# Output projection in seven parts: spilled lo parts by other tiles and another queue, the last part on other banks, norm gains into pages of their own, and a set issue order

## The chip, the cores and the metric

The kernel runs on one core of a Trainium2 chip. TensorE multiplies matrices, VectorE, ScalarE and GpSimd do elementwise work, SyncE (SP) issues most of the DMAs between SBUF, the core's memory, and HBM. The metric is the time of one execution on the device in microseconds (us). The profile comes from one execution that a hardware profiler recorded.

## The reference

One layer of a decoder: three token mixers beside each other, merged by gates, and a gated MLP behind them. D_MODEL and SEQ are 1024, D_FF is 2816, all in fp32. Cut to the stretch that matters here:

```python
y_sb, y_ml, y_xa = ...             # three branches, each 1024 x 512
gates = jax.nn.sigmoid(gate_pre).reshape(bsz, seq, N_BRANCH, D_MODEL)
merged = (gates[:, :, 0] * (y_sb @ w_sb_out[l])
          + gates[:, :, 1] * (y_ml @ w_ml_out[l])
          + gates[:, :, 2] * (y_xa @ w_xa_out[l]))
x = x + merged @ w_o[l]
h = _rmsnorm(x, g_ffn[l])
u = _causal_dwconv(h @ w_up[l], ff_conv_w[l], ff_conv_b[l])
u_val, u_gate = jnp.split(u, 2, axis=-1)
x = x + (jax.nn.silu(u_gate) * u_val) @ w_down[l]
```

## The kernel before

Everything is kept transposed: channels on the 128 partitions, sequence along the free axis, in tiles of 128x1024 (or 128x512 halves). An fp32 product is made of three fp32r matmuls (`mm3`, L141 to L144: hi by hi, hi by lo, lo by hi), so each operand is split into hi and lo: `split` (L128 to L130) copies hi on ScalarE and subtracts lo on VectorE, or on an engine that is given. The larger products run in Strassen's manner, seven part products in place of eight, over sums and differences of quarters of the operands.

Tiles come from pools of rotating buffers by tag: `T(shape, "px")` waits until an earlier user of a px buffer is done. Tags that play a part here: raw, whi and wlo (a weight and its hi and lo), px, y, pg, h and U (general pages), `half()` (small tiles, hf in the profile). A scheduler orders the instructions of each engine by priority and by the data they need; each engine then runs its list in that order. `tc.high_priority` moves instructions ahead, `tc.issue_after` holds them behind a given one. PSUM has four tags of two banks each: pj and tr (LONG), pv and z (SHORT).

**The branches (L1115 to L1151).** 24 units i, eight for each of the three branches; b = i // 8. A unit has two halves of 12 matmuls each, accumulated in a bank pj. The weights `w_br` are loaded and split for two units together. VectorE evacuates each half: for branches 1 and 2, L1138 multiplies the bank by the gate, and L1139 adds the result to `merged`. The branch's four input tiles are loaded from y_d into px by SP (L1065) and split into h at the branch's first unit.

**The W_o sums (L1081 to L1099)** run beside branches 1 and 2, one step after each unit from unit 8 on. GpSimd makes the sums and differences of W_o's quarters, in pg (L1084, L1089, L1094, L1097), four for each of two column halves. `spill` (L1076 to L1079) then forms the sum's hi in a px tile on ScalarE, its lo in another px tile on GpSimd (L130), and SP stores the lo in HBM (slo_d, L1079). There are eight spills. Later `sum_w` (L1169 to L1173) makes hi anew on ScalarE and fetches lo from slo_d by a DMA on GpSimd's queue (L1172).

**The seven parts (L1226 to L1311).** `part_product` (L1157) yields after each of its four d; a d is 12 matmuls into one bank, a part 48. L is a quartet of banks on LONG's tags, R one on SHORT's. `grow` (L1186) adds a bank to an output tile (o1u, o2l, o2u, o1l). `squares` (L1195 to L1202) squares an output on ScalarE and adds it up on VectorE; `rstd` (L153 to L159, matmul L158) and `spread` (L161 to L169, matmul L168) turn the sums into a row of factors on all partitions. `gain` (L1208 to L1210) multiplies an output by g_ffn on ScalarE, in place. `keep` (L1188 to L1190) stores an output in x1_d (the profile calls it x_d). Part 6 accumulates on the chain's banks L; part 7 starts a fresh quartet R, so that o1l is grown from both L and R.

**The start of the FFN (L1335 to L1385)** multiplies the differences of the outputs by the second row of factors (L1206), forms operands t2, t3, t1, bl and t4 (L1354, L1363, L1369 and the splits), and runs the first units' parts in turn as operands come ready.

## Time and profile before

| | |
|---|---|
| runs | 1669.21, 1665.27, 1671.01 us; median 1669.21 |
| profiled execution | 1668.87 us, its span 1667.2 us |
| busy share of the span | TensorE 98%, weight loads 80%, VectorE 74%, ScalarE 50%, GpSimd 8% |
| HBM traffic | 159.86 MB read, 58.80 MB written |
| part products L1 to L7 | 939 to 1021 us in the span |

In rows of the profile, L is the line in the kernel before, PE is TensorE, PEld its weight loads, DVE VectorE, ACT ScalarE, POOL GpSimd. `out<-in` names tiles by their tags, with buffer numbers left out. In a timeline's row a bracket holds the idle time just before the instruction and what ended it. The matmuls overlap, so that a row's duration is longer than the step from start to start.

### The profile page before, as it was taken

Reading aid. Unit: us, or ns where it says so; the run is one execution under the profiler, and the core shown is the slowest. Engines: PE = TensorE matmul, PEld = TensorE weight load, DVE = VectorE, ACT = ScalarE, POOL = GpSimd, SP = SyncE. Lnnn points to the kernel's source line nnn. Section 1 sums busy time; section 2 is a strip of 40 time slices with the busy share of each in tenths; the row PEclk is TensorE's granted clock in tenths of the full one; section 3 lists DMA queues with packets and bytes.
Section 4 is the critical chain, followed back from the end, with each engine's and each line's share of the span. In section 5 each row is a group of like instructions: output and inputs, shape, how many; then the busy total and the mean of one; then the engine's idle time right before and its main releaser. Section 6 shows DMA issues by size and latency. Waiting matters only on the chain.

```text
span 1667.2 us, 21227 instructions
## 1 busy us (share of the span) xinstructions
PE 1627.1 (98%) x7959; PEld 1326.9 (80%) x7959; DVE 1234.3 (74%) x1673; ACT 838.5 (50%) x1278; POOL 140.7 (8%) x188
## 2 busy tenths in 40 slices
PE   8999999999999999999978999999999999999999
PEld 4878888888788888888856876788888888888887
DVE  5558888859665666676566868997778877789864
ACT  4557777546554455566222345564455554543431
POOL 1022222020000001000081000000000000000000
PEclk9999999999999999999988999999999999999999
DMA  8421011424325665336866444223222221486131
GB/s 297 149 65 33 26 39 64 174 79 152 116 101 171 190 184 161 118 123 227 269 212 217 124 136 133 83 101 101 77 76 76 85 95 61 161 319 240 41 136 70
DMA packets 102515, 220.05 MB, mean 132 GB/s; under 512 B 13384, under 2 KB 37256, under 8 KB 102412
## 3 DMA queue, kind: packets, MB, share of 16 engines
q1 hardware_dynamic: 101260, 214.50, 38.0%
q0 software_dynamic: 1152, 4.19, 1.0%
q8 instruction: 63, 1.03, 0.3%
q14 instruction: 40, 0.33, 0.1%
HBM read 159.86 MB, written 58.80 MB: 131 GB/s over the span
## 4 chain that ended last, share of the span: by engine, by line
PE 89%; DMA 4%; DVE 3%; ACT 2%; POOL 1%; issue 1%; SPq 0%; ACTq 0%; POOLq 0%; DVEq 0%
PE ps_pj L142 13%; PE ps_pj L143 12%; PE ps_pj L144 12%; PE ps_pv L144 5%; PE ps_pv L143 5%; PE ps_pv L142 5%; PE ps_tr L144 4%; PE ps_tr L142 4%; PE ps_tr L143 4%; PE ps_z L142 4%; PE ps_z L144 4%; PE ps_z L143 4%; PE ps_pv L440 2%; PE ps_tr L420 2%; PE ps_z L395 1%; PE ps_z L394 1%
## 5 line engine op out<-in xcount | busy, mean ns | idle before, releaser
L143 PE MATMUL ps_pj<-h,whi 128*128 128x512 f32 x520 | 206.1, 396 | 2.2 <-DVE h L130 2.0
L142 PE MATMUL ps_pj<-h,whi 128*128 128x512 f32 x440 | 179.0, 408 | 19.2 <-DVE U L1138 11.7
L129 ACT ACTIVATE whi<-raw 128x512 fp32r<-128x512 f32 (+1 forms) x101 | 82.5, 817 | 154.7 <-PE ps_pj L143 55.1
L144 PE MATMUL ps_pj<-h,wlo 128*128 128x512 f32 x352 | 139.1, 396 | 0.1
L143 PEld LDWEIGHTS ps_pj<-h,whi 128*128 128x128 f32 x520 | 99.0, 190 | 25.1 <-DVE h L130 5.9
L831 DVE SCALAR_TENSOR_TENSOR y<-U,vec,y 128x1023 f32<-128x1023 f32 x88 | 112.5, 1279 | 7.8 <-ACT y L829 7.8
L142 PEld LDWEIGHTS ps_pj<-h,whi 128*128 128x128 f32 x440 | 83.9, 191 | 40.1 <-DVE U L1138 13.3
L408 DVE TENSOR_TENSOR_SCAN U<-U 128x512 f32<-128x512 f32 (+3 forms) x96 | 92.9, 1009 | 22.1 <-POOL U L403 20.5
L142 PE MATMUL ps_pj<-pg,whi 128*128 128x512 f32 x268 | 104.5, 390 | 0.0
L144 PE MATMUL ps_pj<-pg,wlo 128*128 128x512 f32 x248 | 96.7, 390 | 0.0
L144 PEld LDWEIGHTS ps_pj<-h,wlo 128*128 128x128 f32 x352 | 67.2, 191 | 15.0 <-DVE wlo L130 0.6
L130 DVE TENSOR_TENSOR wlo<-raw,whi 128x1024 fp32r<-128x1024 f32 x44 | 54.4, 1235 | 29.4 <-ACT whi L129 29.3
L143 PE MATMUL ps_pv<-h,whi 128*128 128x512 f32 x190 | 73.9, 389 | 0.0
L143 PE MATMUL ps_pj<-pg,whi 128*128 128x512 f32 x188 | 73.4, 390 | 0.0
L129 ACT ACTIVATE whi<-pg 128x512 fp32r<-128x512 f32 (+1 forms) x46 | 35.3, 769 | 62.4 <-PE ps_z L143 18.2
L829 ACT ACTIVATE y<-U,vec 128x1024 f32<-128x1024 f32 x44 | 54.6, 1241 | 17.4 <-DVE U L722 16.9
L144 PE MATMUL ps_pj<-h,whi 128*128 128x512 f32 x160 | 62.6, 391 | 0.0
L144 PE MATMUL ps_pv<-h,wlo 128*128 128x512 f32 x152 | 59.5, 392 | 0.0
L142 PE MATMUL ps_pv<-h,whi 128*128 128x512 f32 x150 | 58.5, 390 | 0.4 <-DVE U L722 0.4
L142 PEld LDWEIGHTS ps_pj<-pg,whi 128*128 128x128 f32 x268 | 50.3, 188 | 10.2
L130 DVE TENSOR_TENSOR wlo<-raw,wlo 128x512 fp32r<-128x512 f32 x55 | 37.8, 687 | 26.6 <-ACT wlo L129 26.2
L397 ACT ACTIVATE U<-ps_z 128x1024 f32<-128x1024 f32 (+3 forms) x48 | 39.1, 814 | 32.0 <-PE ps_z L395 24.1
(492 smaller groups left out, 4550.1 us busy)
## 6 DMA issues: line engine op xcount, KB each, us to landing
raw<-in_w_t_dram SPq DMA_DIRECT2D x29, 512.0 KB
gate_d<-U SPq DMA_DIRECT2D x24, 512.0 KB
U<-gate_d SPq DMA_DIRECT2D x22, 512.0 KB
act_d<-y SPq DMA_DIRECT2D x22, 512.0 KB
pg<-in_w_t_dram SPq DMA_DIRECT2D x21, 512.0 KB
raw<-in_w_dn_dram SPq DMA_DIRECT2D x18, 512.0 KB
h<-act_d SPq DMA_DIRECT2D x14, 512.0 KB
raw<-in_w_br_dram SPq DMA_DIRECT2D x12, 512.0 KB
```

Source lines behind the costliest of these rows:

```text
L129: nc.scalar.activation(hi, src, AF.Copy)
L130: (eng or nc.vector).tensor_sub(lo, src, hi.bitcast(F32))
L142: nc.tensor.matmul(out, lh, rh, start=start, stop=False, skip_group_check=more)
L143: nc.tensor.matmul(out, lh, rl, start=False, stop=False, skip_group_check=more)
L144: nc.tensor.matmul(out, ll, rh, start=False, stop=stop, skip_group_check=more)
L394: nc.tensor.matmul(z[:, a, :w], qs[a][:, ts(rb)], ks[a][:, c], start=True, stop=False)
L397: nc.scalar.activation(f[:, :, 1:w + 1], z[:, :, :w], AF.Sigmoid, scale=-0.125)
L408: nc.vector.tensor_tensor_scan(f[:, a, 1:w + 1], f[:, a, 1:w + 1], f[:, a, 1:w + 1], 1.0 if o == 0 else f[:, a, 0:1], op0=ALU.mult, op1=AL ...
L420: nc.tensor.transpose(pt[:, a, ts(j)], g[:, a, ts(j)], ident)
L440: nc.tensor.matmul(pv[64 * a:64 * a + 64, ts(rb % 4)], sbv[s // 2][:, s % 2, (2 * p + a) * 64:(2 * p + a + 1) * 64], wt[a][:, ts(j)], star ...
L829: nc.scalar.activation(out, u, AF.Identity, bias=bias, scale=taps[0])
L831: nc.vector.scalar_tensor_tensor(out[:, :S - s], u[:, s:], taps[s], out[:, :S - s], op0=ALU.mult, op1=ALU.add)
```

## The change

Six edits, in the stretch from the W_o sums to the FFN's start:

1. `spill` takes its two tiles from tag y in place of px, and GpSimd's queue stores lo in place of SP's.
2. L and R change their banks (L on SHORT, R on LONG), and part 7 goes on accumulating on L in place of a fresh R. o1l is grown from part 7 alone, which holds both.
3. `gain` writes into pages of its own: `full` for the upper outputs, `blg` for o2l. The tile that is stored stays as it is.
4. The rstd matmuls of the upper half come after part 6's d = 1 (before: d = 0) and the spread after d = 3 (before: d = 1); the products with the rows and their splits go from part 6's and part 7's steps into part 7's alone.
5. The first FFN weights are loaded, summed and split ahead of part 6 (before: within part 7).
6. Grows and squares of parts 5 and 7 get priority; the parts' loops are written as `stage` and `ready`, which fetch the next part's weights after d = 1 and after the part (before: at d = 0 and d = 2).

The core of the diff:

```diff
@@ -1074,9 +1074,10 @@
     ws = [[None, None] for _ in range(4)]
 
     def spill(i, j):
-        hi, lo = T([P, S], "px", F32R), T([P, S], "px", F32R)
-        split(ws[i][j], hi, lo, nc.gpsimd)
-        nc.sync.dma_start(slo_d[i, j], lo.bitcast(F32))
+        hi, lo = T([P, S], "y", F32R), T([P, S], "y")
+        nc.scalar.activation(hi, ws[i][j], AF.Copy)
+        nc.gpsimd.tensor_sub(lo, ws[i][j], hi.bitcast(F32))
+        nc.gpsimd.dma_start(slo_d[i, j], lo)
 
     def wo_sums(j):
         a1, a2 = wo_load(0, 0, j, "pg"), wo_load(0, 1, j, "pg")
@@ -1205,68 +1209,77 @@
         v = t.rearrange("p (k r) -> p k r", k=2)
         op(v, v, rows.unsqueeze(1).to_broadcast([P, 2, HALF]))
 
-    def gain(o, i):
+    def gain(dst, o, i):
         for d in range(4):
-            nc.scalar.activation(part(o, d), part(o, d), AF.Copy, scale=col(C_GFFN + 4 * i + d))
-
-
-    L, R = four(LONG[::-1]), four(SHORT)
-    w2, w3, w4, w5, w6, w7 = ([None, None] for _ in range(6))
+            nc.scalar.activation(part(dst, d), part(o, d), AF.Copy, scale=col(C_GFFN + 4 * i + d))
 
     def operand(n, src):
         for j in range(2):
             m[n][j] = fine(src[j], "h")
 
+    L, R = four(SHORT), four(LONG)
+    weights = {1: w1}
+
+    def ready(n, j):
+        if n in (2, 5):
+            t = raw_w(1, n // 5, j)
+        else:
+            t = sum_w({3: 2, 4: 1, 6: 0, 7: 3}[n], j)
+        weights.setdefault(n, []).append(t)
+
+    def stage(n, banks, operand, start, after):
+        for d in part_product(banks, weights[n], operand, start):
+            if n < 7 and d == 1:
+                ready(n + 1, 0)
+            after(d)
+        if n < 7:
+            ready(n + 1, 1)
+
     o1u = out_tiles(0, 1, "U")
     operand("bu", bu)
     operand("t3", al)
-    for d in part_product(L, w1, "au", True):
-        if d % 2 == 0:
-            w2[d // 2] = raw_w(1, 0, d // 2)
-        grow(o1u, L, d)
+    stage(1, L, "au", True, lambda d: grow(o1u, L, d))
     operand("t2", au)
 
     o2l = out_tiles(1, 0, "px")
-    for d in part_product(R, w2, "bu", True):
-        if d % 2 == 0:
-            w3[d // 2] = sum_w(2, d // 2)
-        grow(o1u, R, d)
+    stage(2, R, "bu", True, lambda d: grow(o1u, R, d))
     for j in range(2):
         keep(o1u, 0, 1, j)
         nc.vector.tensor_sub(bu[j], bu[j], au[j])
-
-    R = four(SHORT)
-    for d in part_product(R, w3, "t3", True):
-        if d % 2 == 0:
-            w4[d // 2] = sum_w(1, d // 2)
-            nc.vector.tensor_sub(al[d // 2], bl[d // 2], au[d // 2])
-        grow(o2l, R, d)
+    for j in range(2):
+        nc.vector.tensor_sub(al[j], bl[j], au[j])
+
+    full = [page() for _ in range(4)]
+    blg = [page() for _ in range(2)]
+    R = four(LONG)
+    stage(3, R, "t3", True, lambda d: grow(o2l, R, d))
     operand("t4", bu)
 
     o2u = out_tiles(1, 1, "U")
-    for d in part_product(L, w4, "t2", False):
-        if d % 2 == 0:
-            w5[d // 2] = raw_w(1, 1, d // 2)
+
+    def after4(d):
+        grow(o2u, L, d)
         squares(1, part(o1u, d))
-        grow(o2u, L, d)
+
+    stage(4, L, "t2", False, after4)
     operand("t1", al)
-
-    gain(o1u, 0)
-    for d in part_product(R, w5, "t4", False):
-        if d % 2 == 0:
-            w6[d // 2] = sum_w(0, d // 2)
-        grow(o2u, R, d)
-        squares(1, part(o2u, d))
+    gain(full[:2], o1u, 0)
+
+    def after5(d):
+        with tc.high_priority(offset=SOON):
+            grow(o2u, R, d)
+            squares(1, part(o2u, d))
         if d % 2:
             keep(o2u, 1, 1, d // 2)
+
+    stage(5, R, "t4", False, after5)
     operand("bl", bl)
-
-    full = [page() for _ in range(4)]
-
-    def upper(which, o, j, dst):
-        v = full[which + j].rearrange("p (k r) -> p k r", k=2)
-        nc.vector.tensor_mul(v, o[j].rearrange("p (k r) -> p k r", k=2), urows.unsqueeze(1).to_broadcast([P, 2, HALF]))
-        split(full[which + j], *dst[j])
+    gain(full[2:], o2u, 1)
+    w = (*halves(w_up[0], "me"), *halves(w_up[NF], "h"))
+    early = w, T([P, HALF], "sx"), wide()[:, :HALF]
+    sums(*early)
+    early += (pair("U"),)
+    split(w[0], *early[3])
 
     o1l = out_tiles(0, 0, "y")
     diff = [page("h") for _ in range(2)]
@@ -1274,43 +1287,38 @@
     dbu, bbu = doubles("h")
     minus = small(8)[:, :4]
     nc.vector.tensor_scalar(minus, col(C_GFFN, 4), -1.0, None, op0=ALU.mult)
-    gain(o2u, 1)
-    for d in part_product(L, w6, "t1", False):
-        if d == 0:
-            r = rstd(acc[1], HALF, "z")
+    upper = {}
+
+    def after6(d):
         if d == 1:
-            pr = spread(r, 4, "z")
-            urows = T([P, HALF], "raw")
-            nc.scalar.activation(urows, pr, AF.Copy)
-        if d % 2 == 0:
-            w7[d // 2] = sum_w(3, d // 2)
-        if d > 1:
-            upper(0, o1u, d - 2, dau)
+            with tc.issue_after(last[0].ins):
+                upper["r"] = rstd(acc[1], HALF)
+        if d == 3:
+            with tc.issue_after(last[0].ins):
+                pr = spread(upper["r"], 4)
+            upper["rows"] = half()
+            nc.scalar.activation(upper["rows"], pr, AF.Copy)
         grow(o2l, L, d)
         squares(0, part(o2l, d))
+        nc.scalar.activation(part(blg, d), part(o2l, d), AF.Copy, scale=col(C_GFFN + 4 + d))
         if d % 2:
             keep(o2l, 1, 0, d // 2)
-        grow(o1l, L, d)
-
-    R = four(SHORT)
-    gain(o2l, 1)
-    early = None
-    for d in part_product(R, w7, "bl", True):
-        if d == 0:
-            w = (*halves(w_up[0], "me"), *halves(w_up[NF], "h"))
-            early = w, T([P, HALF], "sx"), wide()[:, :HALF]
-            sums(*early)
-        if d == 2:
-            early += (pair("U"),)
-            split(w[0], *early[3])
-        grow(o1l, R, d)
-        squares(0, part(o1l, d))
-        nc.vector.scalar_tensor_tensor(part(diff, d), part(o1l, d), minus[:, d:d + 1], part(o2l, d), op0=ALU.mult,
+
+    stage(6, L, "t1", False, after6)
+
+    def after7(d):
+        with tc.high_priority(offset=SOON):
+            grow(o1l, L, d)
+            squares(0, part(o1l, d))
+        nc.vector.scalar_tensor_tensor(part(diff, d), part(o1l, d), minus[:, d:d + 1], part(blg, d), op0=ALU.mult,
                                        op1=ALU.add)
         if d % 2:
             keep(o1l, 0, 0, d // 2)
-            upper(2, o2u, d // 2, dbu)
-    x1p = o1l + o2l
+        both(nc.vector.tensor_mul, full[d], upper["rows"])
+        split(full[d], *(dau, dbu)[d // 2][d % 2])
+
+    stage(7, L, "bl", False, after7)
+    x1p = o1l + blg
 
 
     act_d = dtile([NF // 2, 2, P, S], "act_d")
```

How GpSimd's list changes from the first W_o sum to the eighth spill. First before (L1084 to L1097 are sums, L130 is the lo of a spill):

```order
L1084 TENSOR_TENSOR pg_1211_7442<-pg_1210_7440,pg_1211_7442 128x1024
L1089 TENSOR_TENSOR pg_1217_7482<-pg_1217_7482,pg_1211_7442 128x1024
L130 TENSOR_TENSOR px_1216_7478<-pg_1211_7442,px_1215_7477 128x1024
L1094 TENSOR_TENSOR pg_1210_7440<-pg_1210_7440,pg_1217_7482 128x1024
L1097 TENSOR_TENSOR pg_1226_7528<-pg_1226_7528,pg_1217_7482 128x1024
L130 TENSOR_TENSOR px_1225_7524<-pg_1217_7482,px_1224_7523 128x1024
L1084 TENSOR_TENSOR pg_1241_7614<-pg_1240_7612,pg_1241_7614 128x1024
L130 TENSOR_TENSOR px_1231_7564<-pg_1210_7440,px_1230_7563 128x1024
L1089 TENSOR_TENSOR pg_1247_7654<-pg_1247_7654,pg_1241_7614 128x1024
```

The same stretch now, where L1079 is the lo of a spill and the DMAs to slo_d its stores:

```order
L1085 TENSOR_TENSOR pg_1211_7442<-pg_1210_7440,pg_1211_7442 128x1024
L1090 TENSOR_TENSOR pg_1217_7482<-pg_1217_7482,pg_1211_7442 128x1024
L1079 TENSOR_TENSOR y_1216_7478<-pg_1211_7442,y_1215_7477 128x1024
L1095 TENSOR_TENSOR pg_1210_7440<-pg_1210_7440,pg_1217_7482 128x1024
L1080 DMA slo_d_7085<-y_1216_7478 128x1024
L1098 TENSOR_TENSOR pg_1226_7528<-pg_1226_7528,pg_1217_7482 128x1024
L1079 TENSOR_TENSOR y_1225_7524<-pg_1217_7482,y_1224_7523 128x1024
L1080 DMA slo_d_7085<-y_1225_7524 128x1024
L1085 TENSOR_TENSOR pg_1241_7614<-pg_1240_7612,pg_1241_7614 128x1024
L1090 TENSOR_TENSOR pg_1247_7654<-pg_1247_7654,pg_1241_7614 128x1024
L1079 TENSOR_TENSOR y_1231_7564<-pg_1210_7440,y_1230_7563 128x1024
L1095 TENSOR_TENSOR pg_1240_7612<-pg_1240_7612,pg_1247_7654 128x1024
```

The third lo stood behind the first sum of the second column half (L1084) and stands behind two of its sums now; every store is an instruction of GpSimd's own list, behind its lo and ahead of the next.

On ScalarE, the hi parts of the spills, the splits of the branches' weights (whi; 1235 is that of units 12 and 13, 1249 of 14 and 15, 1277 of 16 and 17) and the splits of branch 2's inputs (h). Before:

```order
L129 ACTIVATE whi_1235_7576<-raw_1234_7574 128x1024
L129 ACTIVATE px_1230_7563<-pg_1210_7440 128x1024
L129 ACTIVATE px_1232_7569<-pg_1226_7528 128x1024
L129 ACTIVATE px_1245_7649<-pg_1241_7614 128x1024
L129 ACTIVATE whi_1249_7658<-raw_1248_7656 128x1024
L129 ACTIVATE px_1254_7695<-pg_1247_7654 128x1024
L129 ACTIVATE px_1260_7735<-pg_1240_7612 128x1024
L129 ACTIVATE whi_1277_7772<-raw_1276_7770 128x1024
L129 ACTIVATE px_1262_7741<-pg_1256_7700 128x1024
L129 ACTIVATE whi_1286_7842<-raw_1285_7840 128x1024
L129 ACTIVATE h_1265_7748<-px_1264_7746 128x1024
L129 ACTIVATE h_1268_7754<-px_1267_7752 128x1024
```

Now, with the spills' hi at L1078:

```order
L129 ACTIVATE h_1274_7766<-px_1273_7764 128x1024
L129 ACTIVATE whi_1219_7486<-raw_1218_7484 128x1024
L1078 ACTIVATE y_1215_7477<-pg_1211_7442 128x1024
L1078 ACTIVATE y_1224_7523<-pg_1217_7482 128x1024
L129 ACTIVATE whi_1235_7576<-raw_1234_7574 128x1024
L1078 ACTIVATE y_1230_7563<-pg_1210_7440 128x1024
L1078 ACTIVATE y_1232_7569<-pg_1226_7528 128x1024
L129 ACTIVATE whi_1249_7658<-raw_1248_7656 128x1024
L1078 ACTIVATE y_1245_7649<-pg_1241_7614 128x1024
L1078 ACTIVATE y_1254_7695<-pg_1247_7654 128x1024
L1078 ACTIVATE y_1260_7735<-pg_1240_7612 128x1024
L129 ACTIVATE whi_1277_7772<-raw_1276_7770 128x1024
```

The last two rows before and the first row now are input splits of branch 2: all four went from the end of this stretch to its front. whi_1249 stood behind five hi parts and stands behind four; whi_1277 stood behind seven and still does.

On TensorE, the rstd matmuls of part 6 (L158; in the row, four matmuls are one). Before, with the last matmuls of d = 0 ahead:

```order
L142 MATMUL ps_tr_1322_8073<-h_1381_8397,whi_1383_8417 128x512
L143 MATMUL ps_tr_1322_8073<-h_1382_8398,whi_1383_8417 128x512
L144 MATMUL ps_tr_1322_8073<-h_1381_8397,wlo_1384_8418 128x512
L158 MATMUL ps_z_1412_8523<-ones_79,hf_1321_8072 128x1 x4
L142 MATMUL ps_tr_1323_8074<-h_1379_8393,whi_1383_8417 128x512
L143 MATMUL ps_tr_1323_8074<-h_1380_8394,whi_1383_8417 128x512
L144 MATMUL ps_tr_1323_8074<-h_1379_8393,wlo_1384_8418 128x512
```

Now, with the last matmuls of d = 1 ahead:

```order
L142 MATMUL ps_pv_1323_8074<-h_1387_8403,whi_1390_8439 128x512
L143 MATMUL ps_pv_1323_8074<-h_1388_8404,whi_1390_8439 128x512
L144 MATMUL ps_pv_1323_8074<-h_1387_8403,wlo_1391_8440 128x512
L158 MATMUL ps_tr_1422_8558<-ones_79,hf_1321_8072 128x1 x4
L142 MATMUL ps_z_1324_8075<-h_1385_8399,whi_1395_8481 128x512
L143 MATMUL ps_z_1324_8075<-h_1386_8400,whi_1395_8481 128x512
L144 MATMUL ps_z_1324_8075<-h_1385_8399,wlo_1396_8482 128x512
```

The small matmuls moved by 12 places within the part, from bank z to bank tr.

More of the change, by code (lines that the diff above doesn't have):

```diff
@@ L143, in mm3 @@
         nc.tensor.matmul(out, lh, rl, start=False, stop=False, skip_group_check=more)
-        nc.tensor.matmul(out, ll, rh, start=False, stop=stop, skip_group_check=more)
+        return nc.tensor.matmul(out, ll, rh, start=False, stop=stop, skip_group_check=more)
     def rstd_cols(ps_cols, n, width):
@@ L1155, in four @@
         return [bank(t) for t in (tags[0], tags[0], tags[1], tags[1])]
+    last = [None]
     def part_product(banks, w, n, start):
@@ L1162, in part_product @@
                 mh, ml = m[n][k // 2]
-                mm3(banks[d], hi[:, c], lo[:, c], mh[:, hs(k % 2)], ml[:, hs(k % 2)], start and k == 0, k == 3, not start)
+                last[0] = mm3(banks[d], hi[:, c], lo[:, c], mh[:, hs(k % 2)], ml[:, hs(k % 2)], start and k == 0,
+                              k == 3, not start)
             yield d
```

## Prediction

> **What bounds the kernel now.** I read the page first. TensorE bounds the whole, so this change can only win back idle TensorE time and time at a low clock:
>
> ```profile
> PE 1627.1 (98%) x7959; PEld 1326.9 (80%) x7959; DVE 1234.3 (74%) x1673; ACT 838.5 (50%) x1278; POOL 140.7 (8%) x188
> ```
>
> Next the waits of TensorE from 800 us to 1110 us, the stretch that the diff touches. Columns: total us, times, longest:
>
> ```profile
> PE ps_pj L142 <- DVE U L1138: 11.7, 3, 10.3
> PE ps_pj L142 <- ACT h L129: 7.5, 4, 5.6
> PE ps_pj L143 <- DVE h L130: 2.0, 3, 1.3
> PE ps_pj L144 <- DVE U L130: 1.5, 1, 1.5
> ```
>
> The windows tell where. After the length come PE, PEld, DVE, ACT and POOL, each busy us and count, then granted clock, DMA share and GB/s:
>
> ```profile
> 840.00:860.00 20.00, 13.58 (x58) 10.16 (x56) 12.90 (x9) 2.84 (x3) 18.96 (x8) 0.99 0.67 226
> 860.00:880.00 20.00, 15.06 (x56) 12.24 (x57) 15.71 (x14) 6.13 (x6) 10.72 (x5) 0.75 0.77 255
> 880.00:900.00 20.00, 13.73 (x39) 8.00 (x38) 10.43 (x10) 5.28 (x5) 2.40 (x1) 0.74 0.79 261
> 920.00:940.00 20.00, 20.00 (x90) 16.57 (x89) 16.44 (x22) 3.63 (x4) 0.00 (x0) 1.00 0.48 145
> 1020.00:1040.00 20.00, 17.42 (x68) 12.77 (x66) 18.30 (x29) 8.31 (x13) 1.42 (x1) 0.91 0.43 144
> 1040.00:1060.00 20.00, 17.39 (x68) 13.99 (x69) 18.53 (x24) 9.36 (x13) 0.00 (x0) 0.91 0.00 1
> ```
>
> An undisturbed stretch (920 to 940) starts a matmul about every 0.227 us, so 12 of them, one half of a unit, take 2.72 us and a part of 48 takes 10.9 us. Two places fall short of that: 840 to 901 us (place A, the W_o sums beside the branch projections) and 996 to 1067 us (place B, from part 6 to the start of the FFN). A matmul that needs 0.227 us at full clock can cost 0.43 us after a stall, as TensorE's own timeline shows at place A (start, duration, instruction, idle before):
>
> ```profile
> 864.94 0.80 PE L142 MATMUL ps_pj<-h,whi 128*128 128x512 f32 x1 [10.29 <-DVE U L1138]
> 870.10 0.40 PE L142 MATMUL ps_pj<-h,whi 128*128 128x512 f32 x1
> 883.51 0.39 PE L144 MATMUL ps_pj<-h,wlo 128*128 128x512 f32 x1
> 889.51 1.22 PE L142 MATMUL ps_pj<-h,whi 128*128 128x512 f32 x2 [5.61 <-ACT h L129]
> 901.20 0.50 PE L142 MATMUL ps_pj<-h,whi 128*128 128x512 f32 x1 [0.33 <-DVE U L1138]
> ```
>
> Twelve matmuls lie between 864.94 and 870.10: 5.16 us, 2.44 too many. Unit 16, the first of branch 2 (24 matmuls, 5.44 us of work), takes from 883.74 to 901.20: 17.46 us, so 12.0 are lost. With the first stall's 10.3 us, place A loses 24.7 us.
>
> The Trainium skill (TensorE: Matmul & The Clock Gate, What's actually happening) has the array at half clock after an idle window of about 3.4 us, with 426.7 ns from start to start at 512 columns. The 5.16 us for 12 agree.
>
> **Place A: what holds TensorE.** The chain that ended last names it (start, length, what):
>
> ```profile
> 858.70 2.31 POOL px L130
> 861.02 2.95 DMA slo_d<-px
> ...
> 875.85 2.40 POOL px L130
> 878.27 2.88 DMA slo_d<-px
> 881.28 2.41 POOL px L130
> 883.71 2.85 DMA slo_d<-px
> 886.63 4.01 DMA px<-y_d
> ```
>
> Spills go one at a time: GpSimd's lo subtraction 2.4 us, store 2.9 us, about 5.4 in all. And branch 2's inputs (px<-y_d) wait for the spills' last px tiles, which is the second stall. The first stall is ScalarE's order: the weight split for units 14 and 15 stands behind the hi copy of the fifth spill, and that behind GpSimd's fourth lo; on VectorE an evacuation of unit 12, whose bank TensorE wants for unit 13, stands behind that split's lo part (ScalarE's rows, then VectorE's):
>
> ```profile
> 861.03 1.06 ACT L129 ACTIVATE px<-pg 128x1024 fp32r<-128x1024 f32 x1 [6.69 <-POOL px L130]
> 861.99 1.04 ACT L129 ACTIVATE whi<-raw 128x1024 fp32r<-128x1024 f32 x1
> 863.06 1.23 DVE L130 TENSOR_TENSOR wlo<-raw,whi 128x1024 fp32r<-128x1024 f32 x1 [9.27 <-ACT whi L129]
> 864.20 0.68 DVE L1138 SCALAR_TENSOR_TENSOR U<-U,ps_pj 128x512 f32<-128x512 f32 x1
> ```
>
> From that hi copy (861.03) to TensorE's restart (864.94) it is 3.9 us.
>
> **Place A after the change.** The spills leave px, so branch 2's four loads and splits move up beside units 4 to 7, and the second stall goes: 12.0 us less. But a store by GpSimd's queue replaces SP's in the serial chain, and by ScalarE's new order the weights of units 14 and 15 wait for hi 4 (GpSimd's lo 3), those of 16 and 17 for hi 7, so for lo 6. I step through GpSimd's new order with durations from before, starting at the third lo:
>
> ```profile
> 850.69 2.55 POOL L130 TENSOR_TENSOR px<-pg,px 128x1024 fp32r<-128x1024 f32 x1 [0.27 <-DMA slo_d<-px]
> ```
>
> Lo 3 ended at 853.24. One more sum (a subtraction of the same size, 2.35 us by the lo rows above) and two DMA issues (0.53 each, row below) now stand ahead of it, so it ends at about 856.7. The first stall then ends 3.95 us later, at 860.6 instead of 864.94: it stays, 4.3 us shorter. Call the time from issue to landing of a store l. Lo 4, 5 and 6 each wait for the store before: lo 6 ends 2.35 + 3 x 2.4 + 3 l = 9.6 + 3 l after lo 3, and hi 7, the split of unit 16's weights and the evacuation of unit 14 behind its lo part take 4.5 us more (as 3.9 above, and two hand-overs): TensorE starts unit 15 at 856.7 + 14.1 + 3 l. From there it needs 5.16 + 3 x 2.72 = 13.3 us to the end of unit 16: 884.1 + 3 l, against 901.20. So a new stall arises ahead of unit 15, and its size hangs on l. The trace has no store by GpSimd's queue. Nearest are that queue's reads of the same 512 KB, in the lines of slo_d:
>
> ```profile
> L1172 POOL DMA_DIRECT2D wlo<-slo_d x8: 527/530/808, 956.2 to 1010.5; - x8
> ...
> DMA to landing us min/median/max: 3.7/4.6/5.0
> ```
>
> Ends: the hardware queue's stores (2.9) and the slowest of these reads (5.0). By 2.9 place A gains 8.4, by 5.0 it gains 2.1. A hardware read of this size takes 4.0 (886.63, above) and a software one 4.6, so I add that 0.6 to a hardware store's 2.9: l = 3.5, and place A ends at 894.6, a gain of 6.6. The Trainium skill (DMA: Bandwidth & Descriptors, Anatomy of one DMA — SWDGE (gpsimd) path) has 2.0 us plus bytes over 436 thousand, for 512 KB an estimate of 3.2; by it the gain would be 7.5, and no store here shows it.
>
> Against this stand the four input splits, early in units 4 to 7, on engines that also evacuate: VectorE's four lo parts cost 1.23 each (the row at 863.06) in front of evacuations. Bounds: nothing, if they fall into VectorE's idle time, or 4.9. I take 2.6, about half, which also takes in a later first sum, since four loads of 512 KB now go ahead of the W_o loads on SP's queue. Place A gains 4.0, from -3 to 8.
>
> **Place B after the change.** In-place gain is what delays the squares: gain overwrites the tile that is being stored, so ScalarE waits for the store, and squares and weight splits queue behind it. The chain's rows, then TensorE's:
>
> ```profile
> 989.30 5.38 DMA x_d<-U
> ...
> 1004.60 5.79 DMA x_d<-px
> ```
>
> ```profile
> 998.35 1.05 PE L158 MATMUL ps_z<-ones,hf 128*128 128x1 f32 x8 [1.65 <-DVE hf L1202]
> ...
> 1003.69 0.59 PE L168 MATMUL ps_z<-hf,ones 128*128 128x512 f32 x1
> ...
> 1020.91 0.39 PE L142 MATMUL ps_pj<-pg,U 128*128 128x512 f32 x1
> ...
> 1043.10 0.50 PE L143 MATMUL ps_pj<-h,whi 128*128 128x512 f32 x1 [1.29 <-DVE h L130]
> ```
>
> Separate pages take that wait away, and the rstd matmuls come 24 - 12 = 12 matmuls later (2.7 us), more than the 1.65 they wait. That saves the 1.65, and behind it 1.7 at low clock (the 12 matmuls from 999.26, after the eight small ones, to 1003.69 take 4.4 instead of 2.72): part 7 ends at about 1017.5 instead of 1020.91, 3.4 earlier. The spread stands after another 24 matmuls (5.4 us) and is hidden. The first FFN weights are split ahead of part 6, so the wait of 1.5 (L144 <- DVE U L130) goes.
>
> From there VectorE sets the pace, as the rows 1020 to 1060 show (18.3 and 18.5 of 20). The last part on the chain's banks removes four grows:
>
> ```profile
> 1023.15 0.68 DVE L1186 SCALAR_TENSOR_TENSOR y<-ps_z,y 128x512 f32<-128x512 f32 x1
> ...
> 1036.09 2.35 DVE L1206 TENSOR_TENSOR h<-h,ps_tr 128x1024 f32<-128x1024 f32 x2 [1.37 <-PE ps_tr L168]
> ```
>
> With a start every 0.60 us or so these are 2.4 us, and the two early FFN splits take 1.2 more out of the dense stretch. The first product with the lower rows started at 1036.09; at 3.4 + 2.4 less I place it about 5.3 earlier, not 5.8, since the four gains into pages for o2l fall to ScalarE ahead of the splits. The waits behind it (L142 <- ACT h, L143 <- DVE h, 1.3 each, and their slow stretches) shift with it. By the end of t1's product, some 30 us later, about 6.5 should be left: the 5.3 and 1.2 of slow clock. Bounds: only the DVE work taken away, 2 (if the rest meets a later store or split), and 10, when most goes of the 12 that B loses by these rows (5.2 idle from 1020 to 1060, 3.6 there at a clock of 0.91, 3.4 behind 996).
>
> The order of banks L and R, `half` for the rows and the return value of mm3 have one answer: nothing, except that part 7 now waits for part 6's banks. Those are read by VectorE with priority (0.68 each) and a bank comes up again 36 matmuls later (8.2 us), so this is covered.
>
> **Sum.** 1668.87 (the profiled execution; span 1667.2) - 4.0 - 6.5 = 1658.4. The three runs have their median at 1669.21, 0.3 away. Runs of before differ by up to 5.7 us, so 0.3%, 5 us, is about what can be told from no change.
>
> **Rivals.**
> 1. The spill chain on GpSimd's queue decides (l = 5.0, the slowest read). Place A then gains 2.1 - 2.6, nothing, and only B is left: 1662.4. For it: every spill waits for the store before. Chance 0.17, half of it faster by over 0.3%.
> 2. B stays bound by VectorE: the removed 2.4 are refilled by the page writes' order, B gives 2 to 3, in all 1662.5. For it: VectorE's 90% there. Chance 0.15, half of it within 0.3%.
> 3. Both go well: l = 2.9, early splits in idle time, B 8: 1668.87 - 8.4 - 8 = 1652.5. Chance 0.10.
> 4. Slower: VectorE keeps GpSimd from making a store's descriptors, so that l grows to 9. That VectorE and GpSimd slow each other is in VectorE's rows, without and beside a GpSimd operation:
>
> ```profile
> 829.31 0.69 DVE L1139 TENSOR_TENSOR pg<-pg,U 128x512 f32<-128x512 f32 x1
> ...
> 845.99 2.18 DVE L1139 TENSOR_TENSOR pg<-pg,U 128x512 f32<-128x512 f32 x1
> ```
>
> At l = 9 place A ends at 911.1, 9.9 late, and with 2.6 for the splits loses 12.5: 1668.87 + 12.5 - 6.5 = 1674.9. Place A and B cancel at l = 7, and from 8.7 it is slower by over 0.3%. Against it: issues on this queue took 0.53 us (0.81 at most) and landed within 5.0. Chance 0.10. This is the rule of the Trainium skill that speaks against the change (SBUF — State Buffer, SBUF: two separate sides): a DMA from GpSimd's queue starves for descriptors while VectorE holds the shared port, and it advises the SP queue. The reads here don't show it.
>
> **How the numbers follow.** The forecast has 0.48. Faster: 0.48 + 0.10 + 0.085 + 0.075 = 0.74; same 0.16; slower 0.10. The range leaves out the slower case and the far end of rival 3: from 1651 (l = 2.9 with B at 9.5) to 1667 (A -3 with B 5).
>
> **What would show it.** Right: branch 2's px loads issued ahead of the W_o loads, no wait on h from ScalarE near 885, a stall of 5 to 10 us on L1138 that ends near 881 (856.7 + 14.1 + 3 x 3.5) with twelve slow matmuls, stores landing in about 3.5, no L158 wait, part 7's end 3 us closer to part 6's start. Wrong: stores at 5 or more, TensorE waiting in units 4 to 7 for over 3 us, VectorE's first product with the lower rows less than 3 us earlier after place A is taken off.

## The result, and the profile after

The changed kernel ran in 1663.03 us (median of 8 runs, 1659.68 to 1667.47), before in 1669.36 (8 runs, 1665.27 to 1673.65): a ratio of 0.9962, 95% interval [0.9947, 0.9978]. It is 6.3 us faster. The forecast, 1658.4, lies 11.0 below that median and 10.5 below before's profiled execution. The profiled execution's span is 1661.8 us, 5.4 less than before's.

The page of after: TensorE has 6 us less busy time at the same number of matmuls, since fewer ran at low clock (the granted clock is 0.994 over the whole span, before 0.990); the shares are as they were, but for GpSimd's 9% in place of 8%.

```profile
PE 1621.1 (98%) x7959; PEld 1325.5 (80%) x7959; DVE 1227.1 (74%) x1669; ACT 837.7 (50%) x1278; POOL 144.4 (9%) x196
```

TensorE's waits of after, 790 to 1110 us (total, times, longest):

```profile
PE ps_pj L142 <- DVE U L1139: 18.1, 3, 8.4
PE ps_pj L142 <- ACT h L129: 1.7, 1, 1.7
PE ps_pj L143 <- DVE h L130: 1.3, 1, 1.3
PE ps_pj L142 <- DVE pg L1137: 1.2, 1, 1.2
```

The wait for branch 2's inputs is gone (before, 6.1 of the 7.5 us for ScalarE's h; the rest lay at the FFN's start, as the 1.7 here does), and the wait for evacuations, 11.7 before, is 18.1. (Lines behind `spill` have moved on by one: L1139 is the evacuation L1138 of before.) The windows of after show the same trade:

```profile
820.00:840.00 20.00, 20.00 (x89) 16.35 (x88) 14.20 (x15) 4.00 (x4) 4.91 (x2) 1.00 0.94 326
840.00:860.00 20.00, 17.73 (x72) 14.12 (x70) 12.15 (x12) 3.07 (x3) 15.93 (x9) 0.91 0.80 277
860.00:880.00 20.00, 12.57 (x46) 9.89 (x45) 9.57 (x9) 3.06 (x3) 15.02 (x8) 0.74 0.40 130
880.00:900.00 20.00, 11.56 (x44) 9.11 (x43) 9.71 (x11) 5.18 (x5) 9.44 (x8) 0.83 0.38 138
...
1020.00:1040.00 20.00, 18.01 (x78) 13.41 (x77) 19.05 (x27) 9.67 (x13) 1.40 (x1) 1.00 0.16 54
1040.00:1060.00 20.00, 16.15 (x69) 12.44 (x68) 20.00 (x26) 9.21 (x14) 0.00 (x0) 1.00 0.08 22
```

At place A 840 to 860 is better than before, 860 to 900 is worse. At place B TensorE idles as long as before (5.8 of 40 us against 5.2), but at full clock, 1.00 against 0.91.

Four moments of the profiled executions, from the timelines: when VectorE begins to evacuate branch 1, when TensorE starts part 1, when it has ended part 7, and the span.

| kernel | branch 1 | part 1 starts | part 7 ends | span |
|---|---|---|---|---|
| before | 828.59 | 939.42 | 1020.91 | 1667.2 |
| after | 831.72 | 940.43 | 1018.39 | 1661.8 |

In these two executions the changed kernel has lost 1.0 us up to part 1; from there to the end it wins 6.4. The forecast had a gain of 4.0 and one of 6.5. So the question to the runs is place A.

The three stalls of TensorE at place A in after, ScalarE's rows behind the last, and GpSimd's list, with its first row in before ahead:

```profile
847.56 0.50 PE L142 MATMUL ps_pj<-h,whi 128*128 128x512 f32 x1 [2.27 <-DVE U L1139]
...
867.79 0.79 PE L142 MATMUL ps_pj<-h,whi 128*128 128x512 f32 x1 [7.43 <-DVE U L1139]
...
889.70 0.79 PE L142 MATMUL ps_pj<-h,whi 128*128 128x512 f32 x1 [8.44 <-DVE U L1139]
```

```profile
885.79 1.06 ACT L1078 ACTIVATE y<-pg 128x1024 fp32r<-128x1024 f32 x1 [4.64 <-POOL y L1079]
886.75 1.04 ACT L129 ACTIVATE whi<-raw 128x1024 fp32r<-128x1024 f32 x1
```

```profile
830.66 2.40 POOL L1084 TENSOR_TENSOR pg<-pg,pg 128x1024 f32<-128x1024 f32 x1 [73.90 <-DMA pg<-in_w_o_dram]
```

```profile
835.01 2.40 POOL L1085 TENSOR_TENSOR pg<-pg,pg 128x1024 f32<-128x1024 f32 x1 [77.34 <-DMA pg<-in_w_o_dram]
...
845.77 0.81 POOL L1080 DMA_DIRECT2D slo_d<-y  x1
...
852.78 2.90 POOL L1079 TENSOR_TENSOR y<-pg,y 128x1024 f32<-128x1024 f32 x1 [3.63 <-DMA slo_d<-y]
...
872.45 0.58 POOL L1080 DMA_DIRECT2D slo_d<-y  x1 [0.30 <-POOL y L1079]
877.68 2.38 POOL L1079 TENSOR_TENSOR y<-pg,y 128x1024 f32<-128x1024 f32 x1 [4.66 <-DMA slo_d<-y]
880.36 0.58 POOL L1080 DMA_DIRECT2D slo_d<-y  x1 [0.30 <-POOL y L1079]
883.43 2.33 POOL L1079 TENSOR_TENSOR y<-pg,y 128x1024 f32<-128x1024 f32 x1 [2.50 <-DMA slo_d<-y]
```

A store by GpSimd's queue thus took 7.0 us from its issue to the next lo (845.77 to 852.78), 5.2 (872.45 to 877.68) and 3.07 (880.36 to 883.43). Two explanations offer themselves: VectorE, busy during the first and idle during the third, keeps GpSimd from writing descriptors (theory D, rival 4 of the prediction), or the loads of SP's queue share the DMA engines with the store (theory T). SP's list has them beside the first two:

```profile
843.61 0.34 SPq L1058 DMA_DIRECT2D U<-gate_d  x1
844.04 0.39 SPq L1126 DMA_DIRECT2D raw<-in_w_br_dram  x1
844.52 0.42 SPq L1071 DMA_DIRECT2D pg<-in_w_o_dram  x1
...
872.72 4.91 SPq L1058 DMA_DIRECT2D U<-gate_d  x2
```

### The profile page after: what moved, and what is told of

It reads as the page before. It is cut to its first block, busy times and chain, and to the rows that moved or that the text cites. A ratio compares the mean times of both kernels' runs of the same rounds, so it can differ in the third digit from the quotient of the medians.

```text
span 1661.8 us, 21230 instructions
## 1 busy us (share of the span) xinstructions
PE 1621.1 (98%) x7959; PEld 1325.5 (80%) x7959; DVE 1227.1 (74%) x1669; ACT 837.7 (50%) x1278; POOL 144.4 (9%) x196
## 4 chain that ended last, share of the span: by engine, by line
PE 86%; DMA 5%; DVE 3%; issue 3%; POOL 2%; ACT 2%; SPq 0%; POOLq 0%; DVEq 0%; ACTq 0%
PE ps_pj L142 12%; PE ps_pj L143 12%; PE ps_pj L144 12%; PE ps_pv L142 5%; PE ps_pv L144 5%; PE ps_pv L143 5%; PE ps_tr L142 4%; PE ps_tr L144 4%; PE ps_tr L143 4%; PE ps_z L142 4%; PE ps_z L143 4%; PE ps_z L144 4%; PE ps_pv L440 2%; PE ps_tr L420 2%; DMA raw<-in_w_kv_dram 1%
## 5 line engine op out<-in xcount | busy, mean ns | idle before, releaser
L142 PE MATMUL ps_pj<-h,whi 128*128 128x512 f32 x440 | 178.2, 405 | 19.9 <-DVE U L1139 18.1
L143 PEld LDWEIGHTS ps_pj<-h,whi 128*128 128x128 f32 x520 | 99.3, 191 | 21.1 <-DVE h L130 1.6
L130 DVE TENSOR_TENSOR wlo<-raw,whi 128x1024 fp32r<-128x1024 f32 x44 | 54.4, 1237 | 39.8 <-ACT whi L129 39.7
L130 DVE TENSOR_TENSOR wlo<-raw,wlo 128x512 fp32r<-128x512 f32 x55 | 37.8, 688 | 26.2 <-ACT wlo L129 26.0
```

Of the source, the lines that this page charges most:

```text
L130: (eng or nc.vector).tensor_sub(lo, src, hi.bitcast(F32))
L142: nc.tensor.matmul(out, lh, rh, start=start, stop=False, skip_group_check=more)
L143: nc.tensor.matmul(out, lh, rl, start=False, stop=False, skip_group_check=more)
```

## The experiments

Medians and ratios are against runs of the kernel before on the same chip. Where the text calls a run by its number, these are the numbers: 1 the spill alone, 2 the rest alone, 3 the store on SP's queue, 4 the weights ahead, 5 both cures, 6 VectorE busy, 7 the gains in place, 8 the banks of before, 9 the wider spread, 10 the late FFN weights, 11 the early rstd, 12 the twin.

### The spill alone, and the rest alone

Kernel before with the new `spill` alone:

```diff
-        hi, lo = T([P, S], "px", F32R), T([P, S], "px", F32R)
-        split(ws[i][j], hi, lo, nc.gpsimd)
-        nc.sync.dma_start(slo_d[i, j], lo.bitcast(F32))
+        hi, lo = T([P, S], "y", F32R), T([P, S], "y")
+        nc.scalar.activation(hi, ws[i][j], AF.Copy)
+        nc.gpsimd.tensor_sub(lo, ws[i][j], hi.bitcast(F32))
+        nc.gpsimd.dma_start(slo_d[i, j], lo)
```

> The kernel before with the new spill alone (y tiles, store by GpSimd's queue). Theory 1, from the trace of after: place A as a whole loses about 1.8 us (unit 16 ends at 903.0 in place of 901.2), so 1671, unit 16 ends near 903, stalls of 7 to 9 us on L1138 or L1139. Theory 2, the prediction's: place A gains 4.0, so 1665, and what after lost there comes from something else in the change. Third: 1669, no difference.

Measured: 1667.85 against 1671.16, ratio 0.9983 [0.9974, 0.9993], 3 us faster. In its trace part 1 starts at 939.47, at the same time as before, with the stalls at place A at 2.9, 5.0 and 9.3 us. The second run puts these lines back into the changed kernel, so that the rest of the change stands alone.

> The changed kernel with the old spill (px tiles, store by SP's queue), so that only parts 2 to 6 of the change are in. Theory 1: the whole gain is made from part 6 on, 7 to 8 us: 1661 to 1662, as fast as or faster than after, unit 16 ends near 901. Theory 2 (prediction): 6.5, so 1663, and slower than after by 4 less what place A cost there.

Measured: 1666.25, ratio 0.9973 [0.9962, 0.9985], 4.9 us faster. Part 1 starts at 940.27, and from there to the end it is 722.3 us against 727.8 before, 5.5 less. So place A gains about 3 us by the times (1.2 to 4.3 by the interval, which just takes in the 4.0 forecast) and nothing by its one trace, which at 1669.27 us is slower than that run's median, and the rest gains about 5. The two add up to 8.2, and after's own ratio allows 3.7 to 8.8.

Place A varies from execution to execution. Of the runs below, five keep after's spill and unit order (the busy-VectorE run, and the four that undo one part of place B). Where the first store took 7.0 to 7.8 us (after and two of them), part 1 starts at 940.4 to 942.0; where it took 4.7 to 5.5 us (the other three), at 936.6 to 939.9. Before's one trace has 939.42, so none of them shows the 4.0 us that had been forecast.

### The store on SP's queue

```diff
-        nc.gpsimd.dma_start(slo_d[i, j], lo)
+        nc.sync.dma_start(slo_d[i, j], lo)
```

> The changed kernel, y tiles kept, lo stored by SP's queue. Theory D (GpSimd's queue makes its descriptors late while VectorE works): the first and fourth store land in about 3 to 3.6 us in place of 6.9 and 5.1, the chain of spills is some 6 us shorter, unit 16 ends near 897, 1657. Theory T (traffic of the DMA engines there, 0.94 of their time at 820 to 840 us): the first store lands in 6 to 7 us on this queue too, and the time stays within 2 us of after's, 1661 to 1665.

Measured: 1654.19, ratio 0.9897 [0.9881, 0.9914], 17.0 us faster than before. After, which differs from it in that one word, had gained 6.3. Its part 1 starts at 930.87. TensorE's last stall of after, 8.44 us, is 0.71:

```profile
870.05 0.79 PE L142 MATMUL ps_pj<-h,whi 128*128 128x512 f32 x1 [6.62 <-DVE U L1139]
...
881.67 0.50 PE L142 MATMUL ps_pj<-h,whi 128*128 128x512 f32 x1 [0.71 <-DVE U L1139]
```

SP's list and GpSimd's at the fourth store of this run:

```profile
866.13 0.32 SPq L1080 DMA_DIRECT2D slo_d<-y  x1
866.55 0.38 SPq L1058 DMA_DIRECT2D U<-gate_d  x1
867.02 0.73 SPq L1071 DMA_DIRECT2D pg<-in_w_o_dram  x1
```

```profile
869.16 2.45 POOL L1079 TENSOR_TENSOR y<-pg,y 128x1024 f32<-128x1024 f32 x1 [3.06 <-DMA slo_d<-y]
```

The store took 3.0 us (866.13 to 869.16) although a gate load and a W_o load stand 0.4 and 0.9 us behind it. The time is nearer theory D's forecast (1657) than T's, and beyond both, but another reading of T fits it as well: in one queue the store is ahead of the loads and they wait. The next two runs part them.

### VectorE busy, and a twin of every store

Ten additions with two SBUF inputs each, on VectorE, where it was idle in after; their result is not used. The evacuations of unit 14 and the split of unit 16's weights are held behind them:

```diff
+            if i == 13 and h == 0:
+                scratch = T([P, HALF], "sx")
+                with tc.issue_after(held.ins):
+                    for _ in range(10):
+                        fill[0] = nc.vector.tensor_add(scratch, ws[2][0][:, :HALF], ws[2][0][:, HALF:]).ins
```

> The changed kernel with ten extra additions of 128x512 on VectorE, each with two inputs in SBUF, placed after unit 13's last evacuation, where VectorE was idle and the fifth and sixth store landed in 2.9 us. They compute nothing that is used. Theory D (VectorE holds up the descriptors of GpSimd's queue): these two stores land in 4 to 5 us or more. Theory T (a store is long when a load of another queue shares the DMA engines): they stay at 2.9 to 3.2 us as long as no load lies beside them.

Measured, one run: 1668.45. VectorE's row of the ten, and GpSimd's rows beside it:

```profile
877.02 11.37 DVE L1149 TENSOR_TENSOR sx<-pg 128x512 f32<-128x512 f32 x10
```

```profile
880.25 0.58 POOL L1081 DMA_DIRECT2D slo_d<-y  x1 [0.30 <-POOL y L1080]
883.33 2.33 POOL L1080 TENSOR_TENSOR y<-pg,y 128x1024 f32<-128x1024 f32 x1 [2.50 <-DMA slo_d<-y]
885.96 0.58 POOL L1081 DMA_DIRECT2D slo_d<-y  x1 [0.30 <-POOL y L1080]
889.02 2.37 POOL L1080 TENSOR_TENSOR y<-pg,y 128x1024 f32<-128x1024 f32 x1 [2.49 <-DMA slo_d<-y]
```

With VectorE at work nearly all the time (2.94 of 3.08 us and 2.96 of 3.06), the stores take 3.08 and 3.06 us, as they did beside an idle VectorE. Theory D falls for this kind of instruction, and what VectorE does beside after's long stores is additions and subtractions too, besides the reading of banks. The Trainium skill (SBUF — State Buffer, SBUF: two separate sides) warns of descriptors held up while VectorE runs an operation in a mode that takes both of its ports, for which it names fp32 copies within SBUF. No run here tries such a copy beside a store.

For theory T, every lo is stored a second time, by SP's queue, in a tensor that nobody reads:

```diff
         nc.gpsimd.dma_start(slo_d[i, j], lo)
+        nc.sync.dma_start(twin_d[i, j], lo)
```

> The changed kernel with every lo stored twice, by GpSimd's queue in slo_d and by SP's queue in a second tensor that nobody reads. Theory T (two transfers on two queues share the DMA engines): the fifth and sixth lo, which waited 3.07 us for a store alone, wait 4 to 5 us, and the chain of spills grows by 5 us or more. Theory F (a store has a fixed time that other transfers don't touch): they wait 3.1 to 3.3 us.

Measured, one run: 1675.25; part 1 starts at 949.53. SP's list and GpSimd's from the fourth store on:

```profile
874.66 0.32 SPq L1082 DMA_DIRECT2D twin_d<-y  x1
875.07 0.39 SPq L1059 DMA_DIRECT2D U<-gate_d  x1
875.55 0.73 SPq L1072 DMA_DIRECT2D pg<-in_w_o_dram  x1
```

```profile
874.93 0.58 POOL L1081 DMA_DIRECT2D slo_d<-y  x1 [0.30 <-POOL y L1080]
881.96 2.38 POOL L1080 TENSOR_TENSOR y<-pg,y 128x1024 f32<-128x1024 f32 x1 [6.45 <-DMA slo_d<-y]
884.63 0.58 POOL L1081 DMA_DIRECT2D slo_d<-y  x1 [0.30 <-POOL y L1080]
885.23 2.41 POOL L1100 TENSOR_TENSOR pg<-pg,pg 128x1024 f32<-128x1024 f32 x1
891.70 2.34 POOL L1080 TENSOR_TENSOR y<-pg,y 128x1024 f32<-128x1024 f32 x1 [4.06 <-DMA slo_d<-y]
```

The twin makes SP's loads wait for the lo, so that each store by GpSimd's queue now has three transfers of 512 KB beside it, and takes 7.0 us (874.93 to 881.96; 884.63 to 891.70; the other stores of this run come to 5.6 to 8.2). That is more than T had forecast, and the size that after's first store had, with three loads beside it as well. Theory T holds: alone 3.07, with a gate load 5.2, with three transfers 7.0. The Trainium skill (DMA: Bandwidth & Descriptors, Queues, rings and completion order) says that each DMA engine goes round between the queues that have work for it; these numbers agree.

### The weights ahead of the hi parts

The branches' weights are fetched and split one pair of units earlier in the program; each spill's hi is held behind the newest split on ScalarE (`held[0]`); the steps of the sums lie at units 8 to 18, and one of them is cut in two:

```diff
+        with tc.issue_after(held[0]):
+            nc.scalar.activation(hi, ws[i][j], AF.Copy)
...
+            if i + 2 < 3 * KT:
+                fetch(i + 2)
+            wh, wl = fetched.pop(i)
...
-        if b:
+        for _ in range((8, 9, 10, 12, 13, 14, 14, 16, 17, 18).count(i)):
             next(beside, None)
```

> The changed kernel with the branches' weights fetched and split one pair of units ahead in the program, each spill's hi held behind the newest weight split on ScalarE, and the eight spills spread over units 9 to 18. Theory O (ScalarE's order is what stalls TensorE: the weight splits behind the spills' hi parts): the stalls of 2.3, 7.4 and 8.4 us and some 5 us at low clock go, about 20 in all: 1643. Theory S (the spills' and sums' traffic stalls TensorE in any order): at least half of it stays, 1653 or more.

Measured: 1651.65, ratio 0.9886 [0.9871, 0.9901], 19.5 us faster than before. This is with the store on GpSimd's queue, some of them still 5 us long. Part 1 starts at 927.77, and the longest stall left is

```profile
860.99 0.71 PE L142 MATMUL ps_pj<-h,whi 128*128 128x512 f32 x1 [2.17 <-DVE U L1153]
```

12.7 us of place A went, and not the whole 20 that theory O had forecast; the time lies between the two theories' forecasts, 1643 and 1653. The run also spreads the spills over more units, and how much of the 12.7 us ScalarE's order alone is worth isn't told apart. Both cures together, then:

> Both cures of place A together: weights one pair ahead with the spills' hi parts behind them (as in the fourth run) and the stores on SP's queue (as in the third). The two runs with one cure each were 17.0 and 19.5 us faster than before. Theory O (both remove the same stalls, those of TensorE behind late weight splits): the gains hardly add, 20 to 22 us faster than before. Theory I (independent causes): up to 30 us faster.

Measured: 1652.08, ratio 0.9897 [0.9879, 0.9914], 17.8 us faster than before. That is no more than the cures alone gave, a little less than theory O's 20 to 22 and far from theory I's 30. So once no weight split stands behind a hi part, shorter stores bring nothing that the times show.

In the last version on this line the steps lie at units 8, 9, 11, 13, 14, 14, 16, 17, 19 and 20:

> The fourth run's kernel (weights one pair ahead, hi parts held behind them, GpSimd's queue) with the eight spills spread over units 9 to 20 in place of 9 to 18. What is left of stalls there lies where GpSimd is busy nearly all the time and VectorE's additions take 2.15 us beside it. Theory C (that mutual slowing is what is left): with less of it at once the stalls of 2.2, 1.2 and 1.8 us and their low clock shrink, 2 to 4 us faster than the fourth run, 21 to 24 us faster than before. Theory R (loads of weights and gates are what is left): no change, 18 to 20 us faster than before.

Measured: 1647.91 (1645.1 to 1652.68), ratio 0.9877 [0.9858, 0.9895], 21.1 us faster than before and the fastest of all, but the interval overlaps with the fourth run's. Part 1 starts at 926.19, 1.6 earlier; the stall that was longest remains:

```profile
862.97 0.50 PE L142 MATMUL ps_pj<-h,whi 128*128 128x512 f32 x1 [2.19 <-DVE U L1153]
```

Whether GpSimd's and VectorE's mutual slowing is what is left, as theory C has it, stays open.

### Place B, one part at a time

Each run undoes one part in the changed kernel. Gains of o2u and o2l in place again:

```diff
-    gain(full[2:], o2u, 1)
+    gain(o2u, o2u, 1)
...
         if d % 2:
             keep(o2l, 1, 0, d // 2)
+            for e in (d - 1, d):
+                nc.scalar.activation(part(o2l, e), part(o2l, e), AF.Copy, scale=col(C_GFFN + 4 + e))
```

> The changed kernel with the gains of o2u and o2l written in place again, after the store of the tile. Theory 1 (prediction): ScalarE waits for the stores, 5 to 6 us each, squares and hi copies come late, 3 us slower than after, so only 3 us faster than before. Theory 2: the later place of the rstd matmuls covers this wait, and the time is that of after within 1 us.

Measured: 1665.78, ratio 0.9977 [0.9967, 0.9987], 4 us faster than before and 2 to 3 slower than after, with intervals that overlap. ScalarE's waits for the stores are back, and TensorE waits for the second sum of squares:

```profile
ACT px L1305 <- DMA x_d<-px: 2.9, 2, 2.3
ACT U L1214 <- DMA x_d<-U: 2.5, 2, 1.3
```

```profile
1021.05 1.02 PE L158 MATMUL ps_tr<-ones,hf 128*128 128x1 f32 x8 [1.79 <-DVE hf L1206]
```

The banks of before, with part 7 on a fresh R and four more grows:

```diff
-    L, R = four(SHORT), four(LONG)
+    L, R = four(LONG[::-1]), four(SHORT)
...
+        grow(o1l, L, d)
...
-    stage(7, L, "bl", False, after7)
+    stage(7, R, "bl", True, after7)
```

> The changed kernel with the banks of before: L on LONG, R on SHORT, part 7 on a fresh R, and o1l grown from both quartets (four more grows). Theory 1 (prediction): VectorE sets the pace from part 6 to the FFN's start, so 2.4 us slower than after, 4 us faster than before. Theory 2: VectorE has room in parts 6 and 7, and TensorE or the rstd chain decides: within 1 us of after.

Measured: 1664.57, ratio 0.9966 [0.9955, 0.9977], as fast as after. VectorE's product with the lower rows starts 91.2 us after part 1's start (1029.15 less 937.92), in after 91.1 (1031.54 less 940.43), before 96.7. Theory 2: the four grows had room. They lie in part 6, as the four that the change removed did in before, whose first and last were:

```profile
999.51 0.68 DVE L1186 SCALAR_TENSOR_TENSOR y<-ps_tr,y 128x512 f32<-128x512 f32 x1
...
1014.11 0.68 DVE L1186 SCALAR_TENSOR_TENSOR y<-ps_pj,y 128x512 f32<-128x512 f32 x1
```

The first FFN weights within part 7 again (`sums` at its d = 0, the split at d = 2):

> The changed kernel with the first FFN weights loaded, summed and split within part 7 again. Theory 1 (prediction): the wait of 1.5 on the split returns and 1.2 us of VectorE's work go back into the dense stretch, 2 to 3 us slower than after, 3 to 4 us faster than before. Theory 2: within 1 us of after.

Measured: 1663.98, ratio 0.9965 [0.9952, 0.9978], as fast as after. But the trace shows that the edit moved nothing: from part 1 to 150 us behind it TensorE, VectorE, ScalarE and GpSimd run the same instructions in the same order as in after: the scheduler took the sums and the split forward although they stood later in the program. VectorE's lo of that split stands 49.2 us after part 1's start in both; in before it had stood 83.1 after it (before, after, this run):

```profile
1022.54 0.68 DVE L130 TENSOR_TENSOR U<-me,U 128x512 fp32r<-128x512 f32 x1
```

```profile
989.66 0.69 DVE L130 TENSOR_TENSOR U<-me,U 128x512 fp32r<-128x512 f32 x1
```

```profile
990.62 0.69 DVE L130 TENSOR_TENSOR U<-me,U 128x512 fp32r<-128x512 f32 x1
```

So this run tests neither theory. It does show that the split comes early without the fifth edit, by some other part of the change. The rstd matmuls after d = 0 and the spread after d = 1 again:

```diff
-        if d == 1:
-            with tc.issue_after(last[0].ins):
-                upper["r"] = rstd(acc[1], HALF)
-        if d == 3:
+        if d == 0:
+            upper["r"] = rstd(acc[1], HALF)
+        if d == 1:
```

> The changed kernel with the rstd matmuls after part 6's d = 0 and the spread after d = 1, as before, but with the gains in pages of their own. Theory 1: the place of the rstd matmuls is what saved TensorE's wait; it returns, 1.7 us and as much at low clock, 3 us slower than after. Theory 2: the gains' pages alone had freed ScalarE, the sums of squares are ready at d = 0 too, and the time is after's within 1 us.

Measured: 1662.72, ratio 0.9962 [0.9948, 0.9976], as fast as after. TensorE's row has no wait at d = 0 any more:

```profile
997.65 0.95 PE L158 MATMUL ps_tr<-ones,hf 128*128 128x1 f32 x8
```

## Why the prediction was right or wrong

The sign came out, the stalls that the change removes and makes came out, and so did the size of place B, in part by luck, since its steps were credited wrongly. Of place A's gain of 4.0 nothing shows in the traces. One of the prediction's own signs of being wrong appeared: stores at 5 us or more.

**Place A.** The second stall went, as forecast, and the new stall behind hi 7 came where it was forecast. It ends at 889.70, not at 881.3. The first became shorter (7.43 for 10.29), but not in the way forecast: it ends 2.9 us later than before (867.79 for 864.94) where 4.3 earlier had been forecast, and is shorter only since TensorE came to it 5.7 later. The step that failed is the lo parts' dates, and in three terms:
- Lo 3 should have ended at 856.7 and ended at 863.75 (861.41 + 2.34). The first sum came 4.35 later than before (835.01), since four loads now go ahead of the W_o loads; the prediction had folded that into a flat 2.6. And lo 2 waited 3.6 us for the first store (852.78), which the prediction hadn't counted as a wait at all. The late first sum also made hi 2, and the split of units 12 and 13 behind it, 4.4 us later (843.07 for 838.71): a wait of 1.07 us in before (843.22) became the stall of 2.27 at 847.56, which the prediction didn't step through.
- l was taken as one number, 3.5. It is 3.07 for a store alone and 5.2 to 7.0 beside loads. From lo 3 to lo 6 it came to 22.0 us (863.75 to 885.76) for 20.1 forecast. Rival 1 had the right side of this, with l = 5.0, and its time, 1662.4, lies 0.6 from the median, but for the wrong reason: its row was a slow read, and what makes a store slow is a load beside it. Rival 2's 1662.5 is as near by luck, since place B gave 5 to 6 us and not 2 to 3.
- The price of the early input splits showed as a wait of 1.2 at 808.91 (the waits above) and shorter gaps behind it, branch 1's start 3.1 later. Of that, 0.9 us is no price, since the first branch's evacuations were that much later already (796.85 for 795.95).

Together lo 6 came 9.0 us late and the restart 8.4, so that unit 16 ends at 902.35 (the two units took 12.65 for 13.3) and not at 894.6: 1.2 us behind before's 901.20, where 6.6 ahead of it had been forecast. The comparison that the prediction lacked is with the same tiles and SP's queue. There part 1 starts 9.4 us earlier than with the old spill (930.87 for 940.27, one trace each, both with the rest of the change): the tiles from tag y are worth that much, and the queue takes it back.

**Rival 4.** For this rival a store was to take 9 us, a value that no row gave. The longest of the changed kernel took 7.0, and the busy VectorE of the sixth run left a store at 3.08. It falls for the instructions that run here, as the reads of before had suggested.

**Place B.** 6.4 us in the profiled execution, 4.9 by the times of the second run, for 6.5. VectorE's product with the lower rows starts 5.6 us earlier after part 1's start (91.1 for 96.7), forecast 5.3. VectorE's first row with the lower rows, to be set beside before's at 1036.09:

```profile
1031.54 2.35 DVE L1210 TENSOR_TENSOR h<-h,ps_tr 128x1024 f32<-128x1024 f32 x2
```

But its steps were credited wrongly:
- Parts 1 to 7 became 3.5 us shorter (77.96 for 81.49), forecast 3.4. The prediction laid that to the later rstd matmuls. Taking back either edit leaves most of it: with two of the gains in place and the later rstd the parts took 78.43 (seventh run), with the pages and the early rstd 78.85, of it 0.4 a wait for a lo part from HBM (eleventh run). No run takes back both.
- The four grows (2.4 us) are worth nothing that can be measured (eighth run). The prediction took them out of the stretch from 1020 on, where VectorE was 18.3 and 18.5 of 20 us busy, and read that as a bound. But the row that it shows for them, at 1023.15, is one of part 7's, which remain; those removed lay from 999.51 to 1014.11, where VectorE was 14.8 of 20 us busy. What the early FFN weights (1.2, and the wait of 1.5) are worth is not shown, since the tenth run leaves them early; on VectorE only one lo part of 0.68 us left the dense stretch. The gains' pages are worth 2.8 of the 5.6 us at the lower rows' product (seventh run: 93.9 after part 1's start), since with them the second sum of squares isn't late behind ScalarE's wait for a store. What gives the remaining 2.8 stays open: the banks and the place of the rstd matmuls, each undone alone, cost nothing that can be measured, and the early FFN weights and the sixth edit (priority and loop order) were never undone.
- The waits at the FFN's start didn't shrink: 5.8 us of idle in 40, with a stall of 1.7 and one of 1.3 where 1.4 and 1.3 had been. What went is the low clock, 1.00 for 0.91.

## What to carry to other kernels

When a transfer moves to another queue, ask what it stood in front of: in one queue it is served ahead of the loads issued after it, in two it shares the DMA engines with them, and 3 us become 5 to 7. A slow chain costs time only where something urgent stands behind it in an engine's list, so first put the urgent work ahead of it (here 12.7 us, together with a wider spread of the chain), and then its length may not matter. An engine that is 90% busy isn't thereby the one that comes last: undo each part alone before crediting it. And look in the trace whether the undoing changed the order that runs: a scheduler may put back what the program moved.

## What of the hardware was unexpected

A store of 512 KB by GpSimd's queue takes 3.07 us whether VectorE is idle or adds with hardly a pause (3.08 and 3.06), and 7.0 us with three transfers of SP's queue beside it. A wait of TensorE of 2.27 us (at 847.56) was enough for a stretch at low clock, though only after a good microsecond at full clock: in after the matmuls step by 0.23 us up to 848.82 and by 0.43 from 849.22 to 851.78. It isn't always enough: behind a wait of 2.64 us in the fifth run (at 901.17) no such stretch follows. The Trainium skill (TensorE: Matmul & The Clock Gate, What's actually happening) has the clock fall after an idle window of about 3.4 us; here it fell after less. VectorE's ten additions took 11.37 us beside GpSimd's lo parts, where 0.69 each would make 6.9.
